# Weights at the moving operands' place modulo 256 bytes: one half per feed-forward block, and every eighth half ahead of it

## The chip, the core and the metric

The kernel runs on one core of a Trainium2 chip. The metric is the time of one execution on the device in microseconds (us), as the median of several runs.

The core has engines that run side by side, each with its own queue of instructions: TensorE (PE in the profile, with its weight loads listed apart as PEld), VectorE (DVE), ScalarE (ACT), GpSimd (POOL) and SyncE (SP), which issues nearly all DMAs here. A matmul has a stationary operand, the weights, loaded into the array by an instruction of its own, and a moving operand that streams through. Both are read from SBUF, the on-chip memory with 128 partitions. Results go to PSUM.

## The reference

A decoder block over 512 tokens and a model width of 2048, in float32: one normalised input, one input projection for two groups of attention heads (dilated, and a compressed, selected and windowed one), an output projection, a gated feed-forward layer of width 5632, and a last normalisation.

```python
hn = rmsnorm(h, norm1_g[l])
proj = hn @ w_in[l]
(q_a, k_a, v_a, q_b, k_c, v_c, k_s, v_s, k_w, v_w, g_b) = jnp.split(proj, offsets, axis=-1)
...
mixed = jnp.concatenate([rmsnorm(o_a, grp_norm_a[l]), rmsnorm(o_b, grp_norm_b[l])], axis=-1)
h = h + mixed @ w_out[l]

hn2 = rmsnorm(h, norm2_g[l])
h = h + (jax.nn.silu(hn2 @ w_gate[l]) * (hn2 @ w_up[l])) @ w_down[l]
...
return rmsnorm(h, final_g)
```

## The kernel before

**Three matmuls for one.** The kernel multiplies in float32r. To keep the precision, every operand is split into a high part (rounded to float32r) and a low part (what the rounding left). `mm3` (and `mm` in the feed-forward part) then makes three matmuls: high weights on high activations, high weights on low activations, low weights on high activations. These are the lines L161, L162, L163 and L1001, L1002, L1003 of the profile: the lines that end in 1 and 2 share the high weights, and each of the three loads its weights anew. The activations are the moving operand, 512 tokens wide in the projections and in the down projection, 256 wide in the feed-forward products.

**Halves of weights.** Weights stream from HBM in units of 128 x 1024 (tile `raw`) and are used in halves of 128 x 512, that is four 128 x 128 weights, hence 12 matmuls per half. For each half a `Job` is made. Its `first` step runs on ScalarE and writes the high part into a tile `wh` (L132); its `second` step runs on VectorE and writes the low part into `wl` (L135). Both tiles come from rings of five. `next_half` hands the halves out in the order of the list `jobs`, and `split_to` keeps the splitting one to four halves ahead of TensorE. With one exception (the last phase, below), each half is used once and its ring place comes free.

**Places.** The helper `placed` allocates a tile that is 64 elements (256 bytes) longer than needed and returns the part that begins at a given element. The four constants are `MH, ML, WH, WL = 32, 32, 16, 16`: moving operands (`ah`, `al`, and the feed-forward operands `B11`, `T1`, `B21`, `T4`) begin at byte 128 of their tile, weights in `wh` and `wl` at byte 64. All these tiles have sizes that are multiples of 256 bytes, and so has what is allocated ahead of them in their pools (the tile `wh` has 576 x 4 = 9 x 256 bytes, `ah` 8256 x 4 = 129 x 256). One weight of a half is 512 bytes per partition and one block of a moving operand 1024 or 2048, so weights and moving operands keep these places modulo 256 all through a half: 64 bytes apart. In the attention, weights and moving operands are also 64 bytes apart (queries at `WH`, keys at `MH`; values at `WH`, probabilities at `MH`).

**The course of the kernel.**
- Projections: 136 units, so 272 halves, through `run_unit`: the compression inputs (`pc`), the keys, values and queries (`pp`), with compression weights (`w1_unit`, where the weight ring is the *moving* side) and the attention's steps mixed in, then the output projection (`pab`).
- Feed-forward: 44 blocks of 128 hidden columns. Per block, gate and up projections are made as seven products P1 to P7 of sums and differences of the four quarters (a Strassen scheme, made by `quad_jobs`, run by `product`), each with two halves: 14 halves, 168 matmuls of 256 columns. Block 0 has an order of its own and waits inside for the second normalisation; blocks 1 to 43 run P1, P7, P4, P6, P5, P2, P3.
- Down projection: after every four blocks, 16 halves for one group (`down`, 512 wide) are mixed in between the products of the next block. The list `sched` holds this order.
- Last phase (`last`): the last group's 16 weight halves are used twice, for the first 256 tokens and for the last 256, so they have to be kept. They do not go into the ring: `kept(nb)` gives them room in operands that are no longer needed, the first eight in `ah` and `al` (blocks 0 to 7, which held the operands of P7 and P6), four in `B11`, four in `T1`. They begin at the places of those moving operands, so in this phase weights and moving operands lie at the same place modulo 256. The matmuls of the phase (`pl`) are 256 wide.

Of the kernel before, what the change touches and what calls it, by code (L numbers as in the profile page):

```python
# [12 lines left out]
F32R = mybir.dt.float32r  # L13
# [3 lines left out]
S = 512  # L17
D = 2048
KB = D // 128
# [17 lines left out]
MH, ML, WH, WL = 32, 32, 16, 16  # L37
# [34 lines left out]
def block_kernel(ctx: ExitStack, tc: tile.TileContext, xt, wst, wdn, smalls, wg, w2c, bias, ident_in, out):  # L72
# [5 lines left out]
    base = ctx.enter_context(tc.tile_pool(name="base", bufs=1))  # L78
    wp = ctx.enter_context(tc.tile_pool(name="wp", bufs=1))
    ps = ctx.enter_context(tc.tile_pool(name="ps", bufs=1, space=bass.MemoryType.PSUM))  # L80

    def placed(pool, n, at, **kw):

        return pool.tile([128, n + 64], F32R, **kw)[:, at:at + n]
# [1 line left out]
    sm = base.tile([128, NSM], F32, name="sm")  # L86
    ident = base.tile([128, 128], F32, name="ident")
    ones = base.tile([128, 128], F32, name="ones")
    ah = placed(base, KB * S, MH, name="ah").rearrange("p (a b) -> p a b", b=S)
    al = placed(base, KB * S, ML, name="al").rearrange("p (a b) -> p a b", b=S)  # L90
    dve.memset(ones, 1.0)
    act.activation(ident[:, :1], ones[:, :1], AF.Copy)
    warm = ps.tile([128, 512], F32, tag="misc", name="warm")
# [7 lines left out]
    def load_to(n):  # L101
        while state["dma"] < min(n, len(units)):
            u = state["dma"]
            t = wp.tile([128, 1024], F32, tag="raw", name="raw", bufs=LA)
            for k in range(2 if u < TWO else 1):
                c = slice(512 * k, 512 * k + 512) if u < TWO else slice(0, 1024)
                sp.dma_start(t[:, c], wst[u][:, c])
            raws[u] = t
            state["dma"] += 1

    late = {}
    jobs = []
    todo_b = deque()
    lag = deque()

    def wsplit():
        return (placed(wp, 512, WH, tag="wh", name="wh", bufs=5),
                placed(wp, 512, WL, tag="wl", name="wl", bufs=5))

    class Job:  # L120


        def __init__(self, src, prep=None, post=None, load=None, dst=None):
            self.src, self.prep, self.post, self.load, self.dst = src, prep, post, load, dst

        def first(self):
            if self.load:
                self.load()
            if self.prep:
                self.prep()  # L130
            self.h, self.l = self.dst() if self.dst else wsplit()
            act.activation(self.h, self.src(), AF.Copy)  # L132

        def second(self):
# [4 lines left out]
    def half_of(u, k):  # L139
        return lambda: raws[u][:, 512 * k:512 * k + 512]  # L140

    for u, d in enumerate(units):
        if d[0] != "quad":
            for k in range(2):
                jobs.append(Job(half_of(u, k), load=lambda u=u: load_to(u + 1)))

    n_plain = len(jobs)
    total = n_plain + 14 * FB + KB * NPH
# [95 lines left out]
    def tokens(*accs):  # L244
        return [[a[:, 128 * t:128 * t + 128] for a in accs] for t in range(accs[0].shape[-1] // 128)]
# [46 lines left out]
    for k in range(KB):  # L292
        x = xc.pop(k)
# [128 lines left out]
    def evac(p, tag, scale=None, keep=False):  # L422

        t = tmp()
        if scale is None:
            dve.tensor_tensor(t, p, r1, op=OP.mult)
        else:
            dve.scalar_tensor_tensor(t, p, scale, r1, op0=OP.mult, op1=OP.mult)
        ph, pl = (MH, ML) if tag[0] == "k" else (WH, WL)
        h = placed(kvq(tag), S, ph, tag=tag + "h", name=tag + "h")  # L430
        l = placed(kvq(tag), S, pl, tag=tag + "l", name=tag + "l")
        act.activation(h, t, AF.Copy)
        dve.tensor_tensor(l, t, h.bitcast(F32), op=OP.subtract)
# [213 lines left out]
    def proj_block(upto=None):  # L647
        return ps.tile([128, 512], F32, tag="proj", name="pp", bufs=2)
# [40 lines left out]
    for j in range(NH):  # L689
# [5 lines left out]
        p = proj_block()  # L695
# [8 lines left out]
        p = proj_block()  # L704
# [15 lines left out]
        t = evac_v(p)  # L720
# [14 lines left out]
    def load_fin(n):  # L735
        while len(fin) < min(n, KB // 2):
            k = 2 * len(fin)
            fin.append(wp.tile([128, 1024], F32, tag="raw", name="fin", bufs=LA))
            sp.dma_start(fin[-1].rearrange("p (n c) -> p n c", n=2), wdn[NPH - 1, k:k + 2].rearrange("n p c -> p n c"))

    def quad_jobs(f, order):

        u = base_u + 4 * f

        def q(i, k):
            return raws[u + i][:, 512 * k:512 * k + 512]

        def comb(o, a, b, op):
            return lambda: dve.tensor_tensor(o(), a(), b(), op=op)  # L749

        def nxt(i):
            return lambda: load_to(u + 4 + i + 1)

        r = {}
        for k in range(2):
            A11, A21, A22, A12 = (lambda i=i, k=k: q(i, k) for i in range(4))
            if f == 0:
                def s1(A11=A11, A21=A21, A22=A22):
# [12 lines left out]
            r["P6", k] = Job(A22, prep=comb(A22, A22, A11, OP.subtract))  # L771
            r["P2", k] = Job(A12)
            r["P3", k] = Job(A12, prep=comb(A12, A12, A22, OP.subtract))
        if f + 1 < FB:
            if f == 0:
                r["P6", 1].post = nxt(1)
                r["P3", 1].post = nxt(3)
            else:
                r["P6", 1].post = nxt(0)
                r["P5", 1].post = nxt(1)  # L780
                r["P3", 1].post = nxt(3)
        else:
            r["P6", 1].post = lambda: load_fin(1)
            r["P5", 1].post = lambda: load_fin(2)
            r["P3", 1].post = lambda: load_fin(LA)
        return [r[p, k] for p in order for k in range(2)]

    ORDER0 = ("P1", "P5", "P2", "P7", "P4", "P6", "P3")
# [4 lines left out]

    def kept(nb):
        def f():
            n = nb % 4
            if nb < 8:
                return ah[:, nb, :], al[:, nb, :]
            t = term["B11" if nb < 12 else "T1"]
            return tuple(a[:, 2 * n:2 * n + 2, :].rearrange("p a b -> p (a b)") for a in t)  # L800
        return f

    sched = []
    for f in range(FB):
        qj = quad_jobs(f, ORDER if f else ORDER0)
        p = f // PH - 1
        nb = 0
# [9 lines left out]
    for nb in range(KB):  # L817
        jobs.append(Job(lambda nb=nb: fin[nb // 2][:, 512 * (nb % 2):512 * (nb % 2) + 512], dst=kept(nb),
                        post=(lambda nb=nb: load_fin(nb // 2 + LA + 1)) if nb % 2 else None))
# [11 lines left out]
    def close_attention():  # L831

        side_hook[0] = lambda: None

        def norms():
            r = rest["r"] = Rsqrt(tokens(acc[:, 0, :]) + tokens(acc[:, 1, :]), NH * HD)
            r.invert()

        def turn_a():
            rest["a"] = Spread(rest["r"].z[:, :4])  # L840

        def turn_q():
            r = rest["r"]
            rest["a"] = rest["a"](False, "o")
            dve.tensor_tensor(r.z[:, 4:], r.y[:, 4:], r.z[:, :4], op=OP.mult)
            rest["q"] = Spread(r.z[:, 4:])

        def close():
            rest["q"] = rest["q"]()
            attn.close()  # L850
            ffn = rest["ffn"] = ctx.enter_context(tc.tile_pool(name="ffn", bufs=1))
            for name in ("B11", "T1", "B21", "T4"):
                term[name] = tuple(placed(ffn, 2048, at, name=name + x).rearrange("p (a b) -> p a b", b=256)
                                   for x, at in (("h", MH), ("l", ML)))
            rest["hs"] = ffn.tile([128, KB, S], F32, name="hs")
            for nb in range(KB):
                sp.dma_start(rest["hs"][:, nb, :], xt[nb])
            for nb, p in pab:
                later(nb // 2, lambda nb=nb, p=p: add_b(nb, p))

        for i in range(8):
            later(i // 2, lambda i=i: split_act(8 + i, osb[:, i, :], sm[:, SM_GA + i:SM_GA + i + 1]))
        for n, f in zip(CLOSE, (norms, turn_a, turn_q, close)):
            later(n, f)
# [13 lines left out]
    term = {}  # L878
    pab = []
    for nb in range(KB):  # L880
        while "hs" not in rest and (nb == 4 and not idle() or nb == 2 and (queue or cur["s"])):
            step()
        p = out_unit(1, ("proj", "sc", "t")[nb // 2 % 3])
# [4 lines left out]
    rab, hs, ffn = rest["r"], rest["hs"], rest["ffn"]  # L888
# [81 lines left out]
    for i in range(KB):  # L970
        nb = PASS2[i]
        p = out_unit(0)
# [96 lines left out]
    for kind, a, b in sched:  # L1069
# [162 lines left out]
```

## Time and profile before

| | |
|---|---|
| median of 3 runs | 2225.5 us (2195.83, 2225.5, 2225.71) |
| the profiled execution | 2224.25 us, span from first to last instruction 2222.5 us |
| mean granted TensorE clock | 0.997 |
| instructions in the span | 35,893 |
| split on ScalarE, `wh` from `raw` | 888 of 628 ns |
| split on VectorE, `wl` from `raw` | 888 of 685 ns |
| combinations of quarters on VectorE (L749) | 352 of 686 ns |
| HBM read | 223.94 MB, 103 GB/s over the span |

A row of the grouped views reads: line of the code, engine, operation, output from inputs by the program's names, shapes, number of instructions; then busy time in us and the mean duration of one in ns; then the engine's idle time just before them and what ended it. Matmuls overlap, so the duration of one is longer than the distance between two starts; the time that a matmul costs is that distance.

### The profile page before, as it was taken

What the parts mean: (1) busy time and instruction counts of PE and PEld (TensorE: products, weight loads), DVE (VectorE), ACT (ScalarE), POOL (GpSimd) and SP (SyncE); (2) the same over time, 40 slices, a digit from 0 to 9 for tenths busy, and PEclk for the clock granted to TensorE, in tenths of its full rate; (3) what the DMA queues carried; (4) which work ended last, traced back from release to release, by engine and by line L of the source; (5) the groups of instructions that cost most, each with busy time, mean ns of one, the idle gap of its engine ahead of it and who ended that gap; (6) DMA issues with size and microseconds to landing.
All of it is one profiled execution on the core that took longest, in us unless ns stands there. A gap on an engine that the chain in (4) does not pass through costs nothing.

```text
span 2222.5 us, 35893 instructions
## 1 busy us (share of the span) xinstructions
PE 2201.1 (99%) x13856; PEld 1981.3 (89%) x13856; DVE 1577.6 (71%) x3051; ACT 969.4 (44%) x1861; POOL 39.5 (2%) x46
## 2 busy tenths in 40 slices
PE   9999999999999999999999999999999999999997
PEld 7788888888878889989898999999898999999897
DVE  6755566365667689878586877768596867778685
ACT  6544444244453355435253443434253434434356
POOL 0000000000000000000000000000000000000003
PEclk9999999999999999999999999999999999999999
DMA  6432222322224232333323332333333232333233
GB/s 219 149 129 79 88 79 68 106 79 79 88 76 161 95 95 79 104 94 115 114 89 107 109 104 87 115 95 110 100 113 101 91 114 96 110 100 103 88 115 104
DMA packets 82252, 230.47 MB, mean 104 GB/s; under 512 B 8736, under 2 KB 13216, under 8 KB 82080
## 3 DMA queue, kind: packets, MB, share of 16 engines
q1 hardware_dynamic: 82080, 228.17, 32.2%
q8 instruction: 109, 1.79, 0.3%
q14 instruction: 63, 0.52, 0.1%
HBM read 223.94 MB, written 4.19 MB: 103 GB/s over the span
## 4 chain that ended last, share of the span: by engine, by line
PE 96%; DVE 2%; ACT 1%; issue 0%; DMA 0%; SPq 0%; DVEq 0%; ACTq 0%
PE P L1003 13%; PE P L1002 13%; PE P L1001 13%; PE pp L161 6%; PE pp L163 6%; PE pp L162 6%; PE pd L162 4%; PE pd L161 4%; PE pd L163 4%; PE P L162 3%; PE P L161 3%; PE P L163 3%; PE pab L161 3%; PE pab L163 3%; PE pab L162 2%; PE pt L510 1%
## 5 line engine op out<-in xcount | busy, mean ns | idle before, releaser
L132 ACT ACTIVATE wh<-raw 128x512 fp32r<-128x512 f32 x888 | 548.1, 628 | 547.8 <-PE P L1002 206.8
L135 DVE TENSOR_TENSOR wl<-raw,wh 128x512 fp32r<-128x512 f32 x888 | 598.9, 685 | 78.6 <-ACT wh L132 69.2
L1003 PE MATMUL P<-ah,wl 128*128 128x256 f32 x1056 | 296.2, 281 | 0.2 <-DVE wl L135 0.2
L1001 PE MATMUL P<-ah,wh 128*128 128x256 f32 x1056 | 295.1, 279 | 0.0
L1002 PE MATMUL P<-al,wh 128*128 128x256 f32 x1056 | 294.9, 279 | 0.0
L161 PE MATMUL pp<-ah,wh 128*128 128x512 f32 x640 | 259.1, 405 | 0.0
L163 PE MATMUL pp<-ah,wl 128*128 128x512 f32 x640 | 251.3, 393 | 0.0
L162 PE MATMUL pp<-al,wh 128*128 128x512 f32 x640 | 250.4, 391 | 0.0
L749 DVE TENSOR_TENSOR raw<-raw 128x512 f32<-128x512 f32 x352 | 241.3, 686 | 3.5
L132 ACT ACTIVATE wh<-rawd 128x512 fp32r<-128x512 f32 x160 | 101.2, 633 | 284.0 <-PE pd L162 162.4
L1002 PEld LDWEIGHTS P<-al,wh 128*128 128x128 f32 x1056 | 198.9, 188 | 0.8
L1003 PEld LDWEIGHTS P<-ah,wl 128*128 128x128 f32 x1056 | 198.5, 188 | 0.5 <-DVE wl L135 0.4
L1001 PEld LDWEIGHTS P<-ah,wh 128*128 128x128 f32 x1056 | 197.9, 187 | 0.9
L1065 DVE TENSOR_TENSOR hs<-hs,pd 128x512 f32<-128x512 f32 x98 | 67.4, 687 | 134.6 <-PE pd L163 134.5
L162 PE MATMUL pd<-al,wh 128*128 128x512 f32 x392 | 154.4, 394 | 0.0
L161 PE MATMUL pd<-ah,wh 128*128 128x512 f32 x392 | 153.7, 392 | 0.0
L163 PE MATMUL pd<-ah,wl 128*128 128x512 f32 x392 | 152.1, 388 | 0.0
L163 PEld LDWEIGHTS pp<-ah,wl 128*128 128x128 f32 x640 | 120.2, 188 | 26.4
L162 PEld LDWEIGHTS pp<-al,wh 128*128 128x128 f32 x640 | 120.6, 188 | 19.7
L161 PEld LDWEIGHTS pp<-ah,wh 128*128 128x128 f32 x640 | 120.6, 188 | 19.6
L135 DVE TENSOR_TENSOR wl<-rawd,wh 128x512 fp32r<-128x512 f32 x160 | 109.7, 686 | 23.4 <-ACT wh L132 22.8
L499 ACT ACTIVATE e<-e,st 128x512 f32<-128x512 f32 (+1 forms) x96 | 54.1, 563 | 133.7 <-DVE st L497 133.7
(277 smaller groups left out, 4934.7 us busy)
## 6 DMA issues: line engine op xcount, KB each, us to landing
raw<-in_wst_dram SPq DMA_DIRECT2D x311, 512.0 KB, 3.5
rawd<-in_wdn_dram SPq DMA_DIRECT2D x160, 256.0 KB, 2.6
bias<-in_bias_dram SPq DMA_DIRECT2D x16, 320.0 KB, 3.0
xc<-in_xt_dram SPq DMA_DIRECT2D x16, 256.0 KB, 2.7
hs<-in_xt_dram SPq DMA_DIRECT2D x16, 256.0 KB, 5.4
fin<-in_wdn_dram SPq DMA_DIRECT2D x8, 512.0 KB, 3.8
out_dram<-hs SPq DMA_DIRECT2D x10, 256.0 KB, 2.2
out_dram<-hs SPq DMA_DIRECT2D x3, 512.0 KB, 3.4
```

What stands on the lines that cost most here:

```text
L132: act.activation(self.h, self.src(), AF.Copy)
L135: dve.tensor_tensor(self.l, self.src(), self.h.bitcast(F32), op=OP.subtract)
L161: pe.matmul(o, wh, mh, start=start, stop=False)
L162: pe.matmul(o, wh, ml, start=False, stop=False)
L163: pe.matmul(o, wl, mh, start=False, stop=stop)
L499: act.activation(et, et, AF.Exp, bias=m, scale=-1.0, accum_out=den)
L510: pe.transpose(p[:, 128 * (o + b):128 * (o + b) + 128], self.e[t][:, 128 * b:128 * b + 128], ident)
L749: return lambda: dve.tensor_tensor(o(), a(), b(), op=op)
L1001: pe.matmul(o, wh, mh, start=start, stop=False, skip_group_check=True)
L1002: pe.matmul(o, wh, ml, start=False, stop=False, skip_group_check=True)
L1003: pe.matmul(o, wl, mh, start=False, stop=stop, skip_group_check=True)
L1065: dve.tensor_tensor(hs[:, nb, :], hs[:, nb, :], p, op=OP.add)
```

## The change

Three things change place; nothing is computed in another way.

1. `Job` gets a flag `even`. With it, `wsplit` allocates the half's `wh` and `wl` at `MH` and `ML` and not at `WH` and `WL`. The flag is set for every eighth half of the projections (34 of 272) and for P1's first half in each of the 44 feed-forward blocks.
2. The whole tiles under `ah`, `al`, `B11`, `T1`, `B21`, `T4` are held in a dictionary `slot`, so that other parts of them than the moving operand's can be named.
3. `kept` gives the last phase's weights places that begin at `WH` and `WL` in those tiles: 16 elements lower than before, each reaching 16 elements into the block below.

```diff
-    ah = placed(base, KB * S, MH, name="ah").rearrange("p (a b) -> p a b", b=S)
-    al = placed(base, KB * S, ML, name="al").rearrange("p (a b) -> p a b", b=S)
+    slot = {x: base.tile([128, KB * S + 64], F32R, name="a" + x) for x in "hl"}
+    ah = slot["h"][:, MH:MH + KB * S].rearrange("p (a b) -> p a b", b=S)
+    al = slot["l"][:, ML:ML + KB * S].rearrange("p (a b) -> p a b", b=S)
...
-    def wsplit():
-        return (placed(wp, 512, WH, tag="wh", name="wh", bufs=5),
-                placed(wp, 512, WL, tag="wl", name="wl", bufs=5))
+    def wsplit(even):
+        return (placed(wp, 512, MH if even else WH, tag="wh", name="wh", bufs=5),
+                placed(wp, 512, ML if even else WL, tag="wl", name="wl", bufs=5))
...
-            self.h, self.l = self.dst() if self.dst else wsplit()
+            self.h, self.l = self.dst() if self.dst else wsplit(self.even)
...
-                jobs.append(Job(half_of(u, k), load=lambda u=u: load_to(u + 1)))
+                jobs.append(Job(half_of(u, k), load=lambda u=u: load_to(u + 1), even=len(jobs) % 8 == 0))
...
+        r["P1", 0].even = True
         return [r[p, k] for p in order for k in range(2)]
...
     def kept(nb):
         def f():
-            n = nb % 4
-            if nb < 8:
-                return ah[:, nb, :], al[:, nb, :]
-            t = term["B11" if nb < 12 else "T1"]
-            return tuple(a[:, 2 * n:2 * n + 2, :].rearrange("p a b -> p (a b)") for a in t)
+            t, n = ("", nb) if nb < 8 else ("B11" if nb < 12 else "T1", nb % 4)
+            return tuple(slot[t + x][:, at + 512 * n:at + 512 * n + 512] for x, at in (("h", WH), ("l", WL)))
         return f
...
             for name in ("B11", "T1", "B21", "T4"):
-                term[name] = tuple(placed(ffn, 2048, at, name=name + x).rearrange("p (a b) -> p a b", b=256)
+                for x in "hl":
+                    slot[name + x] = ffn.tile([128, 2048 + 64], F32R, name=name + x)
+                term[name] = tuple(slot[name + x][:, at:at + 2048].rearrange("p (a b) -> p a b", b=256)
                                    for x, at in (("h", MH), ("l", ML)))
```

More of the change, by code (lines that the diff above doesn't have):

```diff
@@ L114, in block_kernel, with __init__ @@
     lag = deque()
-    def wsplit():
-        return (placed(wp, 512, WH, tag="wh", name="wh", bufs=5),
-                placed(wp, 512, WL, tag="wl", name="wl", bufs=5))
+    def wsplit(even):
+        return (placed(wp, 512, MH if even else WH, tag="wh", name="wh", bufs=5),
+                placed(wp, 512, ML if even else WL, tag="wl", name="wl", bufs=5))
     class Job:
-        def __init__(self, src, prep=None, post=None, load=None, dst=None):
-            self.src, self.prep, self.post, self.load, self.dst = src, prep, post, load, dst
+        def __init__(self, src, prep=None, post=None, load=None, dst=None, even=False):
+            self.src, self.prep, self.post, self.load, self.dst, self.even = src, prep, post, load, dst, even
         def first(self):
```

## The prediction

> **What bounds the kernel now.** I read the page first: the busy shares and the chain of waits.
>
> ```profile
> PE 2201.1 (99%) x13856; PEld 1981.3 (89%) x13856; DVE 1577.6 (71%) x3051; ACT 969.4 (44%) x1861; POOL 39.5 (2%) x46
> ...
> PE 96%; DVE 2%; ACT 1%; issue 0%; DMA 0%; SPq 0%; DVEq 0%; ACTq 0%
> ```
>
> TensorE is busy for 99% of the span and carries 96% of the chain that ended last. The kernel is a queue of 13,856 matmuls, so its time is their number times the distance from one start to the next (I call it the pitch). Only what moves a pitch can move the end. The second view is the table of windows, over a stretch that holds nothing but feed-forward products (columns: window, its length, then busy us and instructions of PE, PEld, DVE, ACT and POOL, then clock and DMA).
>
> ```profile
> 992.00:1058.00 66.00, 66.00 (x563) 66.00 (x562) 58.43 (x101) 32.88 (x56) 0.00 (x0) 1.00 0.32 103
> ```
>
> A matmul is shown for about 280 ns, so 2.4 of the 563 reach in from before the window: (563 - 2.4) / 66.00 us gives a pitch of 117.7 ns. The clock is whole, TensorE never pauses, the weight loads fill the stretch as well, and VectorE is at 58.43 / 66.00 = 89%. The third view groups instructions by shape.
>
> ```profile
> L1003 PE MATMUL P<-ah,wl 128*128 128x256 f32 x1056 | 296.2, 281 | 0.2 <-DVE wl L135 0.2
> L1001 PE MATMUL P<-ah,wh 128*128 128x256 f32 x1056 | 295.1, 279 | 0.0
> ...
> L1001 PE MATMUL P<-B11h,wh 128*128 128x256 f32 x352 | 98.2, 279 | 0.0
> ...
> L162 PE MATMUL pl<-al,ah 128*128 128x256 f32 x64 | 18.1, 283 | 0.0
> ...
> L161 PE MATMUL psc<-kah,qah 128*128 128x256 f32 x16 | 4.5, 278 | 0.0
> ```
>
> One shape, 256 moving columns, has different durations. The products P have weights 64 bytes short of their operand's place and show 279 to 281 ns. The last phase, pl, has weights and operand at one place and shows 283. The attention scores psc, 64 bytes apart like P, show 278. The timeline gives the pitches behind these (columns: start, duration, engine, line).
>
> ```profile
> 153.22 0.28 PE L161 MATMUL psc<-ksh,qbh 128*128 128x256 f32 x1
> ...
> 153.92 0.39 PE L161 MATMUL pp<-ah,wh 128*128 128x512 f32 x1
> ...
> 183.17 0.28 PE L161 MATMUL psc<-kah,qah 128*128 128x256 f32 x1
> ...
> 183.85 0.39 PE L161 MATMUL pp<-ah,wh 128*128 128x512 f32 x1
> ...
> 859.21 0.28 PE L1001 MATMUL P<-ah,wh 128*128 128x256 f32 x1
> ...
> 860.38 0.28 PE L1002 MATMUL P<-al,wh 128*128 128x256 f32 x1
> 860.58 0.39 PE L1003 MATMUL P<-ah,wl 128*128 128x256 f32 x1
> 860.80 0.28 PE L1001 MATMUL P<-ah,wh 128*128 128x256 f32 x1
> ...
> 861.71 0.28 PE L1003 MATMUL P<-ah,wl 128*128 128x256 f32 x1
> ...
> 2164.08 0.28 PE L162 MATMUL pl<-al,ah 128*128 128x256 f32 x1
> ...
> 2170.92 0.28 PE L162 MATMUL pl<-al,ah 128*128 128x256 f32 x1
> ```
>
> The six scores from 153.22 take 0.70 us, 117 ns each; the six from 183.17 take 0.68, 113 each. Inside block 0, ten pitches from 859.21 to 860.38 make 117 ns; then the stream is interrupted (860.38 to 860.58), and the eight from 860.80 to 861.71 take 0.91 us, 114 each, in the same product with the same tiles. From 2164.08 to 2170.92 lie 57 pitches of the last phase: 120.0 ns. So the 64-byte placement has two rhythms, a slow one at 117.7 and a fast one that I take as 113.4 (0.68 / 6 and 0.91 / 8, with starts rounded to 10 ns), and the shared place has one at 120.0. An interruption can swap the rhythm, and without one it lasts. It even outlives the 512-wide matmuls:
>
> ```profile
> L162 PE MATMUL pd<-al,wh 128*128 128x512 f32 x392 | 154.4, 394 | 0.0
> L161 PE MATMUL pd<-ah,wh 128*128 128x512 f32 x392 | 153.7, 392 | 0.0
> L163 PE MATMUL pd<-ah,wl 128*128 128x512 f32 x392 | 152.1, 388 | 0.0
> ```
>
> The three lines of the down products keep three different durations, always on the same lines: a pattern of period three that goes on through every feed-forward block. The products P sit at 279 to 281 throughout, so the profiled execution ran the whole feed-forward part in the slow rhythm.
>
> The times bear on this. There are 44 x 14 x 12 = 7,392 product matmuls (1,056 + 4 x 352 on each of three lines); in the fast rhythm they would take 7,392 x 4.3 = 31.8 us less. The three runs are 2195.83, 2225.5 and 2225.71: the low one is 29.7 below the median. I read it as an execution whose feed-forward part fell into the fast rhythm by chance.
>
> **The change part by part.** The profiled execution took 2224.25 us around its span of 2222.5; the median is 1.25 above it. Copies and subtractions stay as many and as large, with the same rings, DMAs and order; the number of matmuls stays.
>
> First, P1's first half of each block moves to the operands' place: 44 x 12 = 528 matmuls from 117.7 to 120.0, +2.3 each, +1.2 us.
>
> Second, every eighth half ahead moves, 34 of 272. Five of them are halves of the compression weights, where the weight ring is the moving side with 4 matmuls per half; 20 matmuls, which I set at nothing (5 us would need 250 ns on each). The other 29 are 512 wide: 29 x 12 = 348 matmuls. No 512-wide matmul of before has the shared place, so the price is bounded: below by the shortest of the three rows above against their mean, 388 - 391.3 = -3.3 ns; above by twice the price at half the width, +4.6. That is -1.1 to +1.6 us. I take +0.8, the 2.3 ns of the nearest measured case.
>
> Third, the last phase's weights move off the operands' place: 384 matmuls (64 x 3 and 32 x 6) from 120.0 to 117.7 (-0.9 us) or to 113.4 (-2.5 us). Their slots begin 16 elements lower and so reach into the block below in the same tile. ScalarE writes the first of them three to four halves ahead, during P2, and the operands reached into belong to P7 and P6, which come before. No new wait. If one came, the ring of five halves behind it covers 3 x 12 x 117.7 ns = 4.2 us.
>
> Fourth, and largest if it comes, the rhythm. Each moved half puts the other placement in for 12 matmuls, 44 times in the feed-forward part, and forces a return to the 64-byte placement. The way in is in the trace, where the last phase follows the products; the way back is not. Its price per block lies between 13 halves in the fast rhythm, 13 x 12 x 4.3 = -0.67 us, and 13 halves at 120.0, 13 x 12 x 2.3 = +0.36 us. I take the fast end: among the 64-byte runs that started anew, both rhythms occur, as grouping the end of each of the two score runs above shows (first that from 183.17, then that from 153.22),
>
> ```profile
> L162 PE MATMUL psc<-kal,qah 128*128 128x256 f32 x2 | 0.6, 276 | 0.0
> ```
>
> ```profile
> L162 PE MATMUL psc<-ksl,qbh 128*128 128x256 f32 x2 | 0.6, 279 | 0.0
> ```
>
> so that 276 ns marks the fast rhythm and 279 to 281 the slow one, and psc's 278 over all is a mixture. The products already are in the slow one, so a new start can only leave it or find it again. Over 44 blocks, 6,864 x 4.3 = -29.5 us.
>
> Would anything else then be late? VectorE's 58.43 us of work would have to fit into 66.00 x 113.4 / 117.7 = 63.6 us, 92%: enough, with little cover for a burst. ScalarE is at half.
>
> Sum in the fast case: 2224.25 + 1.2 + 0.8 - 2.5 - 29.5 = 2194.3, and 1.25 more against the median: 2195.
>
> **A rule against all this.** The last phase's weight loads and the products' differ as the matmuls do:
>
> ```profile
> L1002 PEld LDWEIGHTS P<-al,wh 128*128 128x128 f32 x1056 | 198.9, 188 | 0.8
> ...
> L162 PEld LDWEIGHTS pl<-al,ah 128*128 128x128 f32 x64 | 12.3, 192 | 0.0
> ```
>
> 188 ns against 192, with 117.7 against 120.0 of pitch. The Trainium skill, "TensorE: Matmul & The Clock Gate", Part 2, "Step-by-step: what each phase is for", says that the two reads of TensorE have independent ports, so that loading the next weights takes nothing from the running matmul. By it, placement would cost nothing and the sum would be zero. These rows disagree by 2.3 ns of 118; nothing here shows which part of the path is shared.
>
> **The rivals.**
>
> *The slow rhythm returns after each moved half.* For it: it holds through every change between 256 and 512 columns in the profiled execution. Then only the direct terms count: 2225.5 + 1.2 + 0.8 - 0.9 = 2227. Chance 0.25.
>
> *Blocks alternate or differ.* Half of them fast: 2225.5 + 1.2 + 0.8 - 1.7 - 14.8 = 2211. Chance 0.14.
>
> *Slower: the moved half leaves its own pitch behind.* If the return keeps the overlap of weight read and operand read that the shared place brought, the following halves run at 120 as well: 6,864 x 2.3 = 15.8 us on top of the direct terms, 2242. It decides where the mean pitch after a moved half exceeds 117.7. Against it: the scores and block 0 found 113 or 117 after every interruption. Chance 0.07. Part of it, 0.02, I leave for a disturbed rhythm in the 512-wide matmuls as well, which could go past 2%.
>
> *No effect at all,* since the placement does not act in this ring as it does in the last phase (or the two reads do not meet): 2225. Against it speak the rows above. Chance 0.04.
>
> *The fast rhythm,* my forecast: 0.50. Of this, 0.05 is for the 512-wide matmuls also losing their period of three and staying at the shortest, 388 against 391.3: there are 240 such halves ahead of the feed-forward part (272 less 32 of the compression) and 160 of the down projection, 400 x 12 = 4,800 matmuls; at 3.3 ns that is another 15.8 us, 2179.
>
> **How the numbers follow.** The likeliest case gives 2195, its own range being 2189 (4.5 ns, last phase included) to 2203 (a quarter of the blocks slow). The range reaches up over the mixed case and the slow return, 2188 to 2230, and leaves out the 120 everywhere and the gain in the 512-wide part: 0.12. Against 2225.5, 2% is 44.5 us (2181 and 2270), about what a measurement of this kernel can tell from no change. Faster by more needs the 512-wide part: 0.05. Slower by more: 0.02. Within: 0.93, although the likeliest case is 1.4% down.
>
> **What would show it.** Products P at 276 ns instead of 279 to 281 in 13 of 14 halves, with P1's first half at 283: forecast right. P at 279 to 281 behind the moved halves: the first rival. Two values by block: the mixed case. P at 283 throughout: the slower one. P1's first half like the rest: no effect. The pl groups should fall from 283 to P's value. Idle time on TensorE with VectorE named as releaser would mean that the fast rhythm outran its weights. My forecast is wrong if the return from the shared place keeps the slow rhythm, the one step that no row of before shows.

## The result, and the profile after

The changed kernel takes 2196.12 us (median of 15 executions, 2194.83 to 2198.22). The kernel before, run beside it, takes 2225.5 (15 executions). The ratio is 0.9887 [0.9861, 0.9913]: 29.4 us less, within 2%. The profiled execution took 2198.18 us; its span is 2196.4, against 2222.5.

The medians hide the better half of the result. Before has two values: 13 of these 15 executions took 2223.7 to 2227.0, two took 2195.8 and 2196.2. Over all the runs of this study it was executed 76 times: 23 took 2191.9 to 2197.6, 53 took 2223.7 to 2227.6, none lay between. Every execution of after lies beside the low ones. The change doesn't go below what before sometimes does; it makes the good case the only one. (One consequence for reading: the ratios of e5 to e8 stand against 5 low and 6 high executions of before, those of e9 to e12 against 8 low ones alone, so there the times in us say more than the ratios.)

First the page of after: its span, the busy shares, the chain of waits, and the groups by shape.

```profile
span 2196.4 us, 35893 instructions
...
PE 2174.5 (99%) x13856; PEld 1954.1 (89%) x13856; DVE 1571.6 (72%) x3051; ACT 969.4 (44%) x1861; POOL 39.5 (2%) x46
...
PE 95%; DVE 3%; ACT 1%; issue 0%; DMA 0%; SPq 0%; DVEq 0%; ACTq 0%
...
L1005 PE MATMUL P<-ah,wl 128*128 128x256 f32 x1056 | 292.1, 277 | 0.4 <-DVE wl L137 0.4
L1003 PE MATMUL P<-ah,wh 128*128 128x256 f32 x1056 | 291.9, 276 | 0.0
...
L1003 PE MATMUL P<-B11h,wh 128*128 128x256 f32 x352 | 98.5, 280 | 0.1
L1003 PE MATMUL P<-T4h,wh 128*128 128x256 f32 x352 | 97.3, 276 | 0.0
...
L164 PE MATMUL pl<-al,ah 128*128 128x256 f32 x64 | 17.7, 277 | 0.0
```

(The lines of the matmuls have numbers larger by two in this code: L1003 is the former L1001.) The same instructions, the same bound, and a shorter distance between them. The products on `ah` and `T4`, none of whose halves was moved, fell from 279 to 281 ns to 276 or 277. Those on `B11` are P1's; half of their halves were moved, and 280 is the mean of 283 and 276. The table of windows gives the pitch, over a stretch of products alone as before.

```profile
993.00:1058.00 65.00, 65.00 (x573) 65.00 (x572) 58.55 (x102) 33.65 (x57) 0.00 (x0) 1.00 0.33 106
```

65.00 us / (573 - 2.4) is 113.9 ns, against 117.7. By the recorded starts, a moved half has 120.0 and each of the 13 behind it 113.3, and (120.0 + 13 x 113.3) / 14 is 113.8. VectorE is at 58.55 / 65.00 = 90%, and the products on `ah` wait 0.4 us for `wl` in the whole execution (the row of L1005).

Where the 26.1 us between the two spans went, the timeline by tile shows (columns: count, shortest / median / longest duration in ns, first and last start).

```profile
L1001 PE MATMUL P<-ah,wh x1056: 276/279/561, 851.9 to 2160.7; 128*128 128x256 f32 x176
...
L161 PE MATMUL pl<-ah x64: 278/283/365, 2161.1 to 2196.7; 128*128 128x256 f32 x64
```

```profile
L1003 PE MATMUL P<-ah,wh x1056: 276/276/561, 854.6 to 2136.5; 128*128 128x256 f32 x176
...
L163 PE MATMUL pl<-ah x64: 276/276/366, 2136.9 to 2170.8; 128*128 128x256 f32 x64
```

| stage | before (first fence) | after (second) | difference |
|---|---|---|---|
| ahead of the first product on `ah` (it lies in block 0) | 851.9 us | 854.6 us | +2.7 |
| feed-forward, from there to the first `pl` | 1309.2 | 1282.3 | -26.9 |
| last phase, from its first to its last L161 / L163 | 35.6 | 33.9 | -1.7 |

The feed-forward part carries all of it. The stage ahead, with 34 of its 272 halves moved, became no shorter; the 2.7 us there are looked at below.

How the rhythm turns can be read block by block. These are two windows of after: block 2, then block 3 from the end of its moved half on.

```profile
893.50:912.50 19.00, 19.00 (x163) 19.00 (x163) 18.16 (x32) 10.03 (x18) 0.00 (x0) 1.00 0.36 113
914.90:931.00 16.10, 16.10 (x144) 16.10 (x143) 15.05 (x27) 8.48 (x15) 0.00 (x0) 1.00 0.39 121
```

19.00 us / (163 - 2.4) is 118.3 ns: block 2 had its moved half and went on in the slow rhythm. 16.10 / (144 - 2.4) is 113.7: block 3 turned. The timeline of P1 in block 3 shows the turn itself, with every third start shown; the half up to 914.79 is the moved one, and from 914.91 on the unmoved one runs.

```profile
914.19 0.28 PE L1003 MATMUL P<-B11h,wh 128*128 128x256 f32 x1
...
914.55 0.28 PE L1003 MATMUL P<-B11h,wh 128*128 128x256 f32 x1
...
914.91 0.28 PE L1003 MATMUL P<-B11h,wh 128*128 128x256 f32 x1
...
915.25 0.28 PE L1003 MATMUL P<-B11h,wh 128*128 128x256 f32 x1
...
915.59 0.28 PE L1003 MATMUL P<-B11h,wh 128*128 128x256 f32 x1
...
915.93 0.28 PE L1003 MATMUL P<-B11h,wh 128*128 128x256 f32 x1
```

Three matmuls lie between two such starts: 0.36 us, twice, are 120 ns each, still in the moved half; 0.34 us, three times, are 113. In block 2 the pitches of the moved half were uneven (117 to 124 by the recorded starts) and the slow pattern came back; in block 3 they had become a flat 120 before the half ended. From block 4 to block 43 each moved half has a flat 120.0, and 113.3 follows without exception.

### The profile page after: what moved, and what is told of

Same layout as the page of the kernel before. It is cut to its first block, busy times and chain, and to the rows that moved or that the text cites. A ratio compares the mean times of both kernels' runs of the same rounds, so it can differ in the third digit from the quotient of the medians.

```text
span 2196.4 us, 35893 instructions
## 1 busy us (share of the span) xinstructions
PE 2174.5 (99%) x13856; PEld 1954.1 (89%) x13856; DVE 1571.6 (72%) x3051; ACT 969.4 (44%) x1861; POOL 39.5 (2%) x46
## 4 chain that ended last, share of the span: by engine, by line
PE 95%; DVE 3%; ACT 1%; issue 0%; DMA 0%; SPq 0%; DVEq 0%; ACTq 0%
PE P L1005 12%; PE P L1003 12%; PE P L1004 12%; PE pp L163 6%; PE pp L165 6%; PE pp L164 6%; PE pd L165 4%; PE pd L164 4%; PE pd L163 4%; PE P L165 3%; PE P L164 3%; PE pab L164 3%; PE P L163 3%; PE pab L163 3%; PE pab L165 2%; PE pt L512 1%
## 5 line engine op out<-in xcount | busy, mean ns | idle before, releaser
L1005 PE MATMUL P<-ah,wl 128*128 128x256 f32 x1056 | 292.1, 277 | 0.4 <-DVE wl L137 0.4
L1003 PE MATMUL P<-ah,wh 128*128 128x256 f32 x1056 | 291.9, 276 | 0.0
L163 PE MATMUL pp<-ah,wh 128*128 128x512 f32 x640 | 259.5, 406 | 0.0
L165 PE MATMUL pp<-ah,wl 128*128 128x512 f32 x640 | 251.2, 393 | 0.0
L1003 PEld LDWEIGHTS P<-ah,wh 128*128 128x128 f32 x1056 | 198.3, 188 | 0.8
L1005 PEld LDWEIGHTS P<-ah,wl 128*128 128x128 f32 x1056 | 198.3, 188 | 0.9 <-DVE wl L137 0.8
L165 PE MATMUL pd<-ah,wl 128*128 128x512 f32 x392 | 154.4, 394 | 0.0
L163 PE MATMUL pd<-ah,wh 128*128 128x512 f32 x392 | 152.1, 388 | 0.0
L165 PEld LDWEIGHTS pp<-ah,wl 128*128 128x128 f32 x640 | 120.2, 188 | 26.7
L163 PEld LDWEIGHTS pp<-ah,wh 128*128 128x128 f32 x640 | 120.8, 189 | 19.8
```

Of the source, the lines that this page charges most:

```text
L163: pe.matmul(o, wh, mh, start=start, stop=False)
L165: pe.matmul(o, wl, mh, start=False, stop=stop)
L1003: pe.matmul(o, wh, mh, start=start, stop=False, skip_group_check=True)
L1005: pe.matmul(o, wl, mh, start=False, stop=stop, skip_group_check=True)
```

## The experiments

All kernels are told as differences from after, unless another is named. "Low" is an execution near 2195 or below, "high" one near 2225.

**The three parts alone.** First the feed-forward halves without the others (e1).

```diff
-                jobs.append(Job(half_of(u, k), load=lambda u=u: load_to(u + 1), even=len(jobs) % 8 == 0))
+                jobs.append(Job(half_of(u, k), load=lambda u=u: load_to(u + 1)))
...
-            return tuple(slot[t + x][:, at + 512 * n:at + 512 * n + 512] for x, at in (("h", WH), ("l", WL)))
+            return tuple(slot[t + x][:, at + 512 * n:at + 512 * n + 512] for x, at in (("h", MH), ("l", ML)))
```

> Only the product half P1 of each feed-forward block is moved; the projections and the last phase stay as before. Theory (the moved half hands the products over to the fast rhythm): products at 276 ns from block 3 or 4 on, last phase at 283 ns, 2196 to 2199 us. Rival (the moved halves of the projections set the rhythm on entry): products at 279 to 281 ns as before, 2226 to 2227 us.

Measured: 2197.36 us (2196.05 to 2198.94), ratio 0.9895 [0.9817, 0.9974]. The P1 halves alone give the whole gain. Its profile turned to 113.3 inside block 2 and stayed there. A window of blocks 2 and 3 is the row to compare with the two above: 31.00 us / (275 - 2.4) = 113.7 ns.

```profile
893.00:924.00 31.00, 31.00 (x275) 31.00 (x274) 29.35 (x51) 16.84 (x30) 0.00 (x0) 1.00 0.34 104
```

Next the halves ahead of the feed-forward part alone (e2).

```diff
-        r["P1", 0].even = True
...
-            return tuple(slot[t + x][:, at + 512 * n:at + 512 * n + 512] for x, at in (("h", WH), ("l", WL)))
+            return tuple(slot[t + x][:, at + 512 * n:at + 512 * n + 512] for x, at in (("h", MH), ("l", ML)))
```

> Only every eighth half ahead of the feed-forward part is moved. Theory: the entry into the products is left to the interruptions in blocks 0 and 1, so mostly 2225 us with products at 279 to 281 ns, now and then 2196. Rival (the projections decide): 2196 us in all runs, products at 276 ns.

Measured: 2225.28 us (10 executions, 3 of them low), ratio 0.9995 [0.9936, 1.0053]. This part does nothing that can be measured, and it doesn't decide how the feed-forward part begins: 3 of 10 is about before's own share, as far as ten executions can tell.

Then the last phase's places alone (e3).

```diff
-                jobs.append(Job(half_of(u, k), load=lambda u=u: load_to(u + 1), even=len(jobs) % 8 == 0))
+                jobs.append(Job(half_of(u, k), load=lambda u=u: load_to(u + 1)))
...
-        r["P1", 0].even = True
```

> Only the last phase's weights leave the operands' place. Theory: 384 matmuls from 120.0 to 117.7 ns, about 1 us less, 2224 to 2225 us, products at 279 to 281 ns. Rival (this move decides the result): 2196 us.

Measured: 2224.48 us (10 executions, 3 low), ratio 0.9984 [0.9921, 1.0047], a difference of about 1 us that the interval doesn't separate from none. Its profile shows the last phase at 117.8 ns, the slow rhythm that it inherited from the products.

**Does the rhythm stay once turned?** Moved halves in blocks 22 to 25 only, nothing else moved (e4; the projections and the last phase as in the first of these kernels).

```diff
-        r["P1", 0].even = True
+        r["P1", 0].even = 22 <= f < 26
```

> The product half is moved in blocks 22 to 25 alone; projections and last phase as before. Theory (the fast rhythm, once reached, holds without further moved halves): slow to block 22, fast from block 25 or sooner to block 43, 19 to 21 blocks of 168 matmuls at 4.4 ns less, 14 to 16 us: 2209 to 2212 us. Rival (each block needs its own moved half): a gain in these four blocks at most, 2222 to 2226 us.

Measured: 2210.44 us (10 executions: eight at 2210.1 to 2210.8, two at 2194.0 and 2195.0), ratio 0.9961 [0.9911, 1.0011]. The eight are what a turn in the middle gives: half the blocks, half the gain. None of them was profiled, but a gain in the four blocks alone would be 4 x 13 x 12 x 4.4 = 2.7 us, and 15 were measured. So four moved halves turn the stream, and the 18 blocks behind them keep the fast rhythm without any. The one profiled was one of the two low executions, and it shows the other way in: it turned in block 4, long before any moved half. Two windows of it:

```profile
870.00:925.00 55.00, 54.95 (x464) 54.81 (x465) 51.82 (x92) 29.41 (x50) 0.00 (x0) 1.00 0.32 101
995.00:1050.00 55.00, 55.00 (x488) 55.00 (x487) 51.24 (x90) 28.59 (x49) 0.00 (x0) 1.00 0.36 115
```

54.95 us / (464 - 2.4) is 119.0 ns, with an interruption in it, and 55.00 / (488 - 2.4) is 113.3. Between the two lies the first group of down halves. So a passage through 512-wide matmuls can turn the products as well. I take before's low executions for such ones; none of before's was profiled.

**Every half at the shared place.** Is the price of 120.0 the shared place itself, and what does it cost the 512-wide matmuls, for which I had only bounds? All ring halves are moved (e5).

```diff
-            self.h, self.l = self.dst() if self.dst else wsplit(self.even)
+            self.h, self.l = self.dst() if self.dst else wsplit(True)
...
-            return tuple(slot[t + x][:, at + 512 * n:at + 512 * n + 512] for x, at in (("h", WH), ("l", WL)))
+            return tuple(slot[t + x][:, at + 512 * n:at + 512 * n + 512] for x, at in (("h", MH), ("l", ML)))
```

> Every weight half of the ring and the last phase's weights lie at the operands' place. Theory: products at 283 ns of duration, 120.0 of pitch, in all blocks, 7,392 x 2.3 = 17.0 us more than before; 512-wide matmuls at the 226.6 ns that the moved halves of the output projection show in the changed kernel, against 228.9, 2.3 less on the 2,688 of output and down projection, 6.2 us less, and less than that again in the input projections: 2231 to 2237 us. Rival (the 512-wide matmuls gain nothing in a stream of such halves): 2242 us.

Measured: 2236.28 us (2235.89 and 2236.67), ratio 1.0123 [0.9951, 1.0295]. The groups by shape:

```profile
L1004 PE MATMUL P<-ah,wl 128*128 128x256 f32 x1056 | 299.1, 283 | 0.0
...
L163 PE MATMUL pd<-ah,wh 128*128 128x512 f32 x392 | 152.5, 389 | 0.0
...
L165 PE MATMUL pd<-ah,wl 128*128 128x512 f32 x392 | 152.5, 389 | 0.0
```

All products show 283 (120.0 of pitch). The down products lose their period of three: 389 on each line, where before had 388, 392 and 394. By starts that is 226.7 ns, against a mean of 228.9. At 512 columns the shared place is the better one, by 2.2 ns.

**So give it to the 512-wide halves.** After, with the projections and the down halves moved as well (e6).

```diff
-                jobs.append(Job(half_of(u, k), load=lambda u=u: load_to(u + 1), even=len(jobs) % 8 == 0))
+                jobs.append(Job(half_of(u, k), load=lambda u=u: load_to(u + 1), even=d[0] != "w1"))
...
-        return Job(lambda: dn[p, nb], post=load_dn)
+        return Job(lambda: dn[p, nb], post=load_dn, even=True)
```

> Like the changed kernel, but every 512-wide half lies at the operands' place, those of the down projection too. Theory (each width has the place that suits it, and the shared place hands over to the fast rhythm): products at 276 ns, 512-wide matmuls of output and down projection 2.3 ns shorter, 5.5 to 8 us below the changed kernel, 2188 to 2191 us. Rival (a 512-wide shared half hands over to the slow rhythm): the products between the down halves in every fourth block at 279 to 281 ns, up to 5 us given back, 2192 to 2196 us.

Measured: 2197.40 us (10 executions), ratio 0.9956 [0.9902, 1.001]: no gain over after, and the main expectation missed; the rival's mechanism is what the groups show. Groups in a window with down halves in it (first fence: 937 to 990) and in one without (second: 995 to 1050):

```profile
L165 PE MATMUL pd<-ah,wl 128*128 128x512 f32 x30 | 11.7, 389 | 0.0
...
L1005 PE MATMUL P<-T4h,wl 128*128 128x256 f32 x8 | 2.2, 280 | 0.0
...
L1003 PE MATMUL P<-T4h,wh 128*128 128x256 f32 x8 | 2.2, 279 | 0.0
```

```profile
L1003 PE MATMUL P<-ah,wh 128*128 128x256 f32 x69 | 19.0, 276 | 0.0
```

A 512-wide half at the shared place hands the products to the slow rhythm (279 and 280 between the down halves), and the next P1 half turns them back. By starts they have 117.8 ns there, against 113.3 in after. Ten groups with ten halves each of products between down halves lose 10 x 10 x 12 x 4.4 = 5.3 us; 1,920 down products gain 2.2 ns, 4.2 us. The input projections (`pp`) gained nothing: by starts their mean pitch is 229.9 ns, against 229.2 in before. Their stream is often interrupted by transposes and attention steps; that this is the reason was not tested.

**Only the first blocks.** If the rhythm stays, P1's half need not be moved 44 times. Projections as before, the last phase as in after (e7).

```diff
-        r["P1", 0].even = True
+        r["P1", 0].even = f < 8
```

> Like the changed kernel, but the product half is moved in blocks 0 to 7 alone, and no half of the projections. Theory (the fast rhythm holds by itself once reached): 36 x 12 matmuls at 113.3 in place of 120.0, 2.9 us below the changed kernel, 2192 to 2194 us in all runs. Rival (moved halves are needed all along): the rhythm is lost again in some blocks, 2197 to 2220 us.

Measured: 2193.39 us (ten executions, 2191.61 to 2195.11), ratio 0.9918 [0.9867, 0.997], the median within the range expected. A window behind the eighth block, with no moved half near (its last 0.6 us belong to the first 512-wide matmuls of the next down halves):

```profile
1114.00:1176.00 62.00, 62.00 (x547) 61.92 (x546) 55.93 (x98) 32.80 (x57) 0.00 (x0) 1.00 0.36 112
```

By starts every half of the products from block 8 on has 113.2 to 113.5 ns. The other 36 moved halves of after cost 36 x 12 x 6.7 = 2.9 us and are not needed: after's median minus this one, from another run, is 2.7.

**Other distances.** Are 64 bytes special? Weights 128 bytes short of the operands' place, no half moved (e8).

```diff
-MH, ML, WH, WL = 32, 32, 16, 16
+MH, ML, WH, WL = 32, 32, 0, 0
...
-        r["P1", 0].even = True
```

> No half is moved; all weights lie 128 bytes from the operands' place modulo 256, not 64. Theory (the rhythm comes from where the two reads meet within 256 bytes): a pitch of the products that is neither 113.4 nor 117.7, or one of these alone; the time between 2190 and 2245 us, by 7,392 matmuls at 113 to 120 ns. Rival (only sharing the place matters): both rhythms as before, mostly 2225 us.

Measured: 2250.56 us (two executions), ratio 1.0188 [1.0015, 1.0361], 5.6 us above the upper end that I had given.

```profile
L1004 PE MATMUL P<-ah,wl 128*128 128x256 f32 x1056 | 297.8, 282 | 0.1
...
L163 PE MATMUL pd<-ah,wh 128*128 128x512 f32 x392 | 154.6, 394 | 0.0
...
L165 PE MATMUL pd<-ah,wl 128*128 128x512 f32 x392 | 154.6, 394 | 0.0
```

By starts the products have one of two steady pitches, 118.7 ns in most blocks and 120.0 in blocks 5 to 12, neither of them 113.4 or 117.7, as the theory had it. The 512-wide matmuls have 233.3 in the output projection, the worst so far. Two rhythms in one execution are thus not special to 64 bytes. The same work with the same instructions is 54 us apart between this kernel and after, by place alone.

**Can the entry be aimed?** The traces offered a rule for the way from 512 to 256 columns at 64 bytes. Around the first down halves, the groups of before (942.6 to 945.6 us; first fence, slow products) and of after (945 to 948; second, fast) are:

```profile
L1001 PE MATMUL P<-T4h,wh 128*128 128x256 f32 x5 | 1.4, 279 | 0.0
...
L162 PE MATMUL P<-al,wh 128*128 128x512 f32 x3 | 1.2, 394 | 0.0
L163 PE MATMUL P<-ah,wl 128*128 128x512 f32 x3 | 1.2, 388 | 0.0
...
L161 PE MATMUL P<-ah,wh 128*128 128x512 f32 x2 | 0.8, 392 | 0.0
```

```profile
L1003 PE MATMUL P<-T4h,wh 128*128 128x256 f32 x5 | 1.4, 276 | 0.0
...
L165 PE MATMUL P<-ah,wl 128*128 128x512 f32 x3 | 1.2, 394 | 0.0
L164 PE MATMUL P<-al,wh 128*128 128x512 f32 x2 | 0.8, 392 | 0.0
L163 PE MATMUL P<-ah,wh 128*128 128x512 f32 x2 | 0.8, 388 | 0.0
```

(In these rows the down products behind a product go by its name; the shape tells them apart.) The last 512-wide matmul ahead of the products is the third of a triple: L163 in before, where it is the 388 ns member, L165 in after, where it is the 394 ns member. The lengths always follow each other as 388, 392, 394; which line has which is the phase in which the stretch was entered. So one or two extra 512-wide matmuls ahead of the first group should move the phase. The kernel before, with (this is e9; for the second kernel, e10, 2 in place of the first 1; they write sums that are then overwritten):

```diff
         h, l = next_half()
+        for _ in range(1 if (ph, nb) == (0, 2) else 0):
+            pe.matmul(p, h[:, :128], ah[:, 12, :], start=True, stop=True)
```

> The kernel before with one more 512-wide matmul in the third down half of block 4; what it writes is overwritten by the half's own first matmul, and no weight moves. Theory (the place in the period of three at which a 256-wide run is entered decides the rhythm, and only the entry behind the 394 ns member gives the fast one): executions that were slow enter behind the 392 ns member and stay slow, those that were fast by chance enter behind the 388 ns member and turn slow; so all runs at 2222 to 2226 us and none at 2193 to 2196. Rival (any disturbance draws a rhythm anew, or none does): a share of runs at 2196 us as before, about 3 in 10.

> The same with two more matmuls (0.46 us) at that one place. Theory: executions that were slow enter the next products behind the 394 ns member and turn fast, 6,672 matmuls at 4.4 ns less, 29 us: most runs at 2195 to 2197 us; those that were fast by chance turn slow, 2222 to 2225 us, about 2 or 3 in 10. Rival (a disturbance changes nothing lasting): mostly 2226 us, as before.

Measured: with one, 2225.80 us (four executions, one low), ratio 1.012 [1.0051, 1.019]; with two, 2224.47 (four, one low), ratio 1.0106 [1.0029, 1.0184]. Two extra matmuls did not turn the kernel to the low value: the expectation missed. The trace of the second says why. Its groups in the down halves just ahead of the extra matmuls (first fence) and behind them, into the products (second):

```profile
L163 PE MATMUL pd<-ah,wl 128*128 128x512 f32 x4 | 1.6, 394 | 0.0
L162 PE MATMUL pd<-al,wh 128*128 128x512 f32 x4 | 1.6, 392 | 0.0
L161 PE MATMUL pd<-ah,wh 128*128 128x512 f32 x4 | 1.6, 388 | 0.0
```

```profile
L1001 PE MATMUL P<-T4h,wh 128*128 128x256 f32 x5 | 1.4, 280 | 0.0
L163 PE MATMUL P<-ah,wl 128*128 128x512 f32 x3 | 1.2, 392 | 0.0
...
L161 PE MATMUL P<-ah,wh 128*128 128x512 f32 x2 | 0.8, 394 | 0.0
L162 PE MATMUL P<-al,wh 128*128 128x512 f32 x2 | 0.8, 388 | 0.0
```

This execution came to the extra matmuls with 394 on L163 already, the good phase; they moved it to 392 on L163, and the products came out slow. So the slow products hand over to the wide matmuls in more than one phase, and a fixed number of extra ones can't aim. The rule for the way out held: over ten traces with 64 bytes, uninterrupted entries into products and into the attention's scores were fast behind the 394 ns member in 403 of 403 cases (250 of them products), and slow behind the 388 or 392 ns member in 343 of 343 (256 products). (Counted from the starts: the last wide matmul of an entry has a pitch of 231, 225 or 229 ns; two entries behind another pitch are left out, as are those behind a moved half and those into the compression, where the weight ring is the moving side: of these, 35 came behind a pitch of 231 and none ran at 113.) That is a regularity of the records, not an explanation. I had also expected no low execution with one extra matmul; each kernel had one, not profiled, and 1 of 4 can't be told from before's share. So the rival, that such a disturbance changes nothing lasting, fits both kernels, and how an execution comes to be low stays open.

**The best of it together.** P1's half in the first eight blocks, the output projection (256 matmuls on each of three lines, seldom interrupted; block 0, whose P1 half is moved, follows it) at the shared place, the input projections not moved, the last phase as in after (e11).

```diff
-                jobs.append(Job(half_of(u, k), load=lambda u=u: load_to(u + 1), even=len(jobs) % 8 == 0))
+                jobs.append(Job(half_of(u, k), load=lambda u=u: load_to(u + 1), even=d[0] == "out"))
...
-        r["P1", 0].even = True
+        r["P1", 0].even = f < 8
```

> The product half moved in blocks 0 to 7 alone, and every half of the output projection at the operands' place. Theory: the gain of that run without moved projections (2193.4 us), and 768 matmuls from 229.0 to 227.0 ns of pitch, 1.5 us: 2191 to 2192.5 us in all runs. Rival (the output projection is not bound by its pitch, or hands over a rhythm that is kept): 2193 us or more.

Measured: 2190.99 us (12 executions, 2189.95 to 2192.09), at the lower end of what was expected. Against before's median in the same run, 2224.76, that is 33.8 us or 1.5% less; against its low executions alone the ratio is 0.9991 [0.998, 1.0001], hardly below. It is the shortest of all. A window of its output projection, beside the same of before:

```profile
700.00:840.00 140.00, 140.00 (x619) 115.99 (x618) 99.37 (x184) 55.95 (x111) 0.00 (x0) 1.00 0.34 110
```

```profile
700.00:840.00 140.00, 140.00 (x613) 114.85 (x612) 97.80 (x181) 55.93 (x112) 0.00 (x0) 1.00 0.32 106
```

A 512-wide matmul is shown for 390 ns, 1.7 pitches: 140.00 / (619 - 1.7) is 226.8 ns, 140.00 / (613 - 1.7) is 229.0.

**The other side of the shared place.** Weights 64 bytes above the operands' place modulo 256 (192 below), no half moved (e12).

```diff
-MH, ML, WH, WL = 32, 32, 16, 16
+MH, ML, WH, WL = 32, 32, 48, 48
...
-        r["P1", 0].even = True
```

> No half is moved; all weights lie 64 bytes behind the operands' place modulo 256, not 64 ahead of it. Theory (what counts is where the two reads meet, which has a direction): a pitch of the products other than 113.4 and 117.7, between 113 and 121 ns, 2190 to 2250 us. Rival (only the distance counts): both rhythms as before, 2225 or 2195 us.

Measured: 2210.98 us (two executions), ratio 1.0084 [1.0062, 1.0106].

```profile
L1002 PE MATMUL P<-ah,wh 128*128 128x256 f32 x1056 | 291.8, 276 | 0.0
...
L163 PE MATMUL pd<-ah,wh 128*128 128x512 f32 x392 | 155.0, 395 | 0.0
L164 PE MATMUL pd<-al,wh 128*128 128x512 f32 x392 | 155.0, 396 | 0.0
```

From block 2 on the products have 113.3 ns in every block, with nothing moved, and the 512-wide matmuls 233.3. The pitch is one of the two that I had excluded; the time lies in the expected range only since the 512-wide matmuls became longer. The slow rhythm exists at this place too: in blocks 0 and 1 four and five halves in a row have 117.8 by starts, until an interruption, and so has the last phase behind its last interruption. With two executions, 2210.5 and 2211.5, it stays open whether some would keep it. The products at this place with the 512-wide ones at the shared place (113.3 and 226.7) were not tried.

## Why the prediction held, step by step

The forecast was 2195 us and 2196.12 was measured. The close number owes something to luck: the rows of before showed that a new start can lead into either rhythm, not which of them follows the shared place, and the chance given was 0.50.

**What bounds it.** Held: an unbroken queue of matmuls in which only the pitch counts. The fast pitch, taken as 113.4 from two short stretches, measured 113.3.

**P1's moved half.** 120.0, as the last phase had shown; 528 x 2.2 = +1.2 us, as in the sum.

**The rhythm.** The step that no row of before showed, the return from the shared place, went the way I took: 13 halves of 14 at 113.3. One detail was off. I had priced all 44 blocks as fast; in the profile the first three were mostly not. Blocks 0 and 1 went fast behind their moved halves, for three and five halves, until an interruption brought 117.8 back. In block 2 the moved half ended before its pitch had become a flat 120, and the slow rhythm was back. Where it had, fast followed each time; why, no run shows. That makes 41 blocks x 156 x 4.4 = 28.1 us, and some 0.4 from fast halves in blocks 0 and 1; less the moved halves' 1.2, the feed-forward part should be 27.3 shorter, and it was 26.9.

The first rival (the slow rhythm returns) is what block 2 did, and no more than that. The mixed case didn't occur from block 3 on. The slower rival didn't occur in after; e6 shows that a like thing exists (the shared place at 512 columns hands over the slow rhythm, not 120). "No effect" fell with every run of the P1 halves.

**The 512-wide halves ahead.** The price was wrong within its bounds: I took +2.3 ns each from the 256-wide case, and the shared place is 2.2 ns shorter at 512 columns where the stream is unbroken (e5, e11), and no shorter where it is interrupted (`pp`). The term was +0.8 us; e2 against before gives -0.3 us, with an interval of 13 us to either side that can't hold so small a term. The 2.7 us that after's profiled execution lost ahead of the feed-forward part can't be put down to this term: by the same view, the first product on `ah` started at 852.8 and 853.2 us in the profiles of e3 and e1, which move nothing ahead of it but, in e1, block 0's own half, at 853.1 in e2, which moves the same 34 halves as after, and at 851.9 in before. Single executions differ by a us or more in this stage, and an effect of one us can't be told from that.

**The last phase.** Taken as 2.5 us at 113.4 throughout; 1.7 measured. By starts it begins at 113.3, is interrupted by the last normalisation's sums, and goes on at 117.8 from there, for 137 of its 384 matmuls.

**VectorE's cover.** Held: 90% busy where 92% was estimated, and the products on `ah` wait 0.4 us for `wl` in all.

**The range.** The lower end of the likeliest case, 2189, doesn't follow from what is said to give it: at 4.5 ns instead of 4.3, 6,864 + 384 matmuls are 1.4 us less, which makes 2194.

**The rule against it.** The Trainium skill, "TensorE: Matmul & The Clock Gate", Part 2, "Step-by-step: what each phase is for", has the weight load and the moving operand on independent read ports, so that loading the next weights takes nothing from the running matmul. Read as I read it, that placement would then be free, it doesn't hold for this kernel: in e5, e8 and e12 the same matmuls take 113.3 to 120.0 ns at 256 columns and 226.7 to 233.3 at 512, by the place of the weights alone. Whether it is the two reads that meet, no run shows: the operand of these matmuls stood at byte 128 in every kernel, so the weights' distance from it and their own place were never told apart.

## What to carry to other kernels

When one kernel's executions fall into two groups a per cent apart, look for equal instructions with unequal durations: here 276, 279 and 283 ns for one shape pointed, before any run, to a pitch that depends on place and to a low execution that was worth forcing. Try the places of stationary and moving operand modulo 256 bytes as a parameter, for each width apart: the best place for 256 columns was not the best for 512. And a disturbance that turns a stream into its better rhythm needs to be paid only until it holds; eight moved halves did the work of 44.

## What was unexpected of the hardware

The pitch of back-to-back matmuls with a weight load each, by how far the weights lie from the operand (at byte 128) modulo 256 bytes:

| weights against operand | 256 columns | 512 columns, unbroken |
|---|---|---|
| same place | 120.0 ns | 226.7 |
| 64 below | 117.8 or 113.3 | 228.9 (three lengths in turn) |
| 128 below | 118.7 or 120.0 | 233.3 |
| 64 above | 113.3, ahead of block 2 also 117.8 | 233.3 |

At 64 below, two rhythms last over thousands of matmuls with the same instructions and data, and 30% of before's executions end in the better one. The steady pitches are whole multiples of 6.67 ns, the step from 113.3 to 120.0, or make one over three matmuls, or over five (113.3 = 17, 120.0 = 18, 226.7 = 34, 233.3 = 35, 3 x 117.8 = 53, 3 x 228.9 = 103, 5 x 118.7 = 89 of them). On what the place of the weights acts, and why the last member of the period of three decides what follows, no run here shows.
